# Two heads' attention scores side by side in 64-row halves of TensorE, and softmax sums from a column of ones

## The chip, the cores and the metric

One Trainium2 chip, one of its cores. The metric is the time of one execution on the device in microseconds (us), as the median of several executions. Inside the core five engines run their own instruction lists and wait for each other through semaphores: TensorE (PE in the profile, with its weight loads as PEld), VectorE (DVE), ScalarE (ACT), GpSimd (POOL) and SyncE (SP), from which nearly all DMAs are issued.

## The reference

One encoder block on 1024 tokens of width 1024. A projection gives queries, keys, values and gates for two groups of eight heads of width 64. Group A attends in a 2-D neighbourhood (16 rows by 64 columns of tokens, a window of 8 rows by 16 columns, a learned bias); group B attends in a band of 128 tokens to either side, with rotary positions, two heads of keys and values for eight of queries, and a learned sink logit per head. Both are gated, projected back, added to the input and normalised.

```python
# group A: neighbourhood
s = jnp.einsum('bqhd,biqjhd->bhqij', q_r, k_win).astype(jnp.float32) * scale
s = s + bias.astype(jnp.float32)[None]
p = jax.nn.softmax(s.reshape(B, H, GRID_W, kh * kw), axis=-1).reshape(B, H, GRID_W, kh, kw)
return jnp.einsum('bhqij,biqjhd->bqhd', p.astype(v.dtype), v_win)
...
# group B: band with a sink
s = jnp.einsum('bnqkgd,bnjkd->bnkgqj', qb, k_band).astype(jnp.float32) * (D ** -0.5)
s = jnp.where(valid[None, :, None, None], s, MASK_VALUE)
p = jax.nn.softmax(jnp.concatenate([s, sink_col], axis=-1), axis=-1)[..., :-1]
out = jnp.einsum('bnkgqj,bnjkd->bnqkgd', p.astype(v.dtype), v_band)
...
mixed = jnp.concatenate([y_a * jax.nn.silu(z_a), y_b * jax.nn.silu(z_b)], axis=-1)
y = jnp.einsum('bse,ed->bsd', mixed, w_out[layer])
x = layer_norm(DEEPNORM_ALPHA * x + y, ln_gain[layer], ln_bias[layer])
```

## The kernel before

Everything is float32 outside. For TensorE each operand is split into two float16 parts, a high one and a low one (h and l in the names), and a product of two matrices is made as the sum of high times high, high times low and low times high.

The kernel has three stages. The first (to about 121 us) makes the values `v` and the first six of 21 projections. The second is the attention, 128 units long, and the third, from about 372 us, is the output projection with the normalisation. The change lies in the second stage and in what prepares it.

A unit (`unit_list`) is 128 queries of one head: group B first, then group A; four pairs `p` of heads in each; within a pair the two heads `j`, and for each the eight blocks `t` of 128 queries. Group A's tokens are sorted by column, so that one block is eight columns of 16 rows. A block's keys lie in the two or three blocks around it, so a unit's scores are 128 by 384, or 128 by 256 for the first and the last block (`geom`).

The loop at the end of `hybrid_block` goes over the units; its counter is called a step. In step `i`:

- `stage_qk` (L777) makes the scores of unit `i` in a PSUM bank of four (tag `s`). Of each head there is a `qs` tile whose 128 rows are 64 rows of q's high part and 64 of its low part, and two `ks` tiles: k's high part twice, one over the other, and its low part twice. So two matmuls with all 128 rows contracted give all four products (L797, L798). Then DVE adds bias or mask and takes the row's extreme in one instruction (L805), out of PSUM into one of two `sn` tiles. For group B a DVE copy puts the sink in column 384 of `sn` (L802).
- `stage_exp` (L811) is ACT's exponential, back into the same PSUM bank, with the row sum as a second result (`accum_out`, read by an instruction of its own).
- `stage_tr` of unit `i - 1` scales the probabilities and splits them in a high part (ACT, L829) and a low part (DVE, L830), and SP issues a DMA that transposes both (L833).
- Every fourth step `stage_pv` (L840) multiplies the transposed probabilities of four earlier units with `v`: for each block of keys three matmuls of 64 columns (L856). One step later `stage_on` (L858) divides by the row sums, and `stage_ot` (L868) transposes pairs of heads with TensorE (L876) and multiplies them onto the gate (L879 group B, L882 group A).
- Between them `pump_to` issues matmuls of the remaining 15 projections (`project`, L380), 48 each, as many as `FILL_AT` says for the step, and later the first ones of the output projection (L1002). When a projection is done, its result is copied out of PSUM: `split_q` and `split_k` write the `qs` and `ks` tiles. For each head and half of the tokens that is an ACT instruction (L250 or L252) and a DVE one (L256; for rotary heads POOL, L258) on 64 partitions, and for keys two POOL copies (L298), which fill the other 64 rows. These instructions stand in queues of work (`enq`, `pop`) and are issued a few per step; `need` issues at once what is still missing when a unit begins.

The first stage's `v_part` (L683) splits `v`; group A's goes to DRAM (`vd`) with 256 numbers for a pair of heads, and `gather_v` (L736) fetches it in the order of columns. Within a step the order of the instructions on each engine is the order of these calls; no scheduler changes it.

Of the kernel before, what the change touches and what calls it, by code (L numbers as in the profile page):

```python
# [27 lines left out]
LTT, LPP, BP, BH, BR, ND, NA, NX, F1 = 1, 6, 2, 9, 5, 1, 1, 6, 0.2  # L28
# [7 lines left out]
FILL_AT = [0, 8, 17, 25, 33, 41, 49, 57, 66, 74, 81, 89, 97, 105, 112, 121, 123.5, 126, 128, 131, 136]  # L36
# [5 lines left out]
VA_STEP = (0, 1, 1)  # L42
# [8 lines left out]
BWIN = (0, 256, 640, 896)  # L51
# [4 lines left out]
def hybrid_block(ctx, tc, xT, x, wt, wv, wo, bias, sink, gain, lbias, cos, sin, bmask, out):  # L56
# [15 lines left out]
    vd = dram.tile([4, GW, ROWS, 256], F16, name="vd")  # L72
# [57 lines left out]
    def stk(kind):  # L130
        if kind == "q":
            return tiles["kq"].tile([128, S], F16, tag="qs", name="qs", bufs=4)
        return tiles["kq"].tile([128, S], F16, tag="ks", name="ks", bufs=8)
# [108 lines left out]
    def own(kind, p, j):  # L242
        if (kind, p, j) not in stks:
            stks[kind, p, j] = stk(kind)
        return stks[kind, p, j]
# [16 lines left out]
    def place(t, a, half, by_col):  # L262
        if not by_col:
            return t[a, 512 * half:512 * half + 512]
        return t[a].rearrange("p (c r) -> p c r", r=ROWS)[:, :, 8 * half:8 * half + 8]

    def taken_from(src, a, by_col):
        return src[a].rearrange("p (r c) -> p c r", c=GW) if by_col else src[a]

    def split_q(p, half, src, dep=None):  # L270
        col = dep is None
        ops = []
        prio = 0 if dep is None else 1
        eng = "pool" if dep and clock["step"] is not None else "dve"
        for j in range(2):
            a, o = slice(64 * j, 64 * j + 64), slice(64 - 64 * j, 128 - 64 * j)
            hi, lo = split_hl(lambda j=j, a=a: place(own("q", p, j), a, half, col),
                              lambda j=j, o=o: place(own("q", p, j), o, half, col),
                              taken_from(src, a, col), dep is None, eng)
            o1 = enq("act", hi, dep, prio=prio, after=28 if dep else 0)  # L280
            ops.append(enq(eng, lo, o1, prio=prio, after=32 if dep else 0))
            stk_ops.setdefault((p, j, half), []).append(ops[-1])
        return ops

    def split_k(p, half, src, dep=None):
        col = dep is None
        ops = []
        prio = 0 if dep is None else 1
        eng = "pool" if dep and clock["step"] is not None else "dve"
        for j in range(2):  # L290
            a, o = slice(64 * j, 64 * j + 64), slice(64 - 64 * j, 128 - 64 * j)
            hi, lo = split_hl(lambda j=j, a=a: place(own("kh", p, j), a, half, col),
                              lambda j=j, a=a: place(own("kl", p, j), a, half, col),
                              taken_from(src, a, col), dep is None, eng)

            def dup_(w, j=j, a=a, o=o):
                t = own(w, p, j)
                nc.gpsimd.tensor_copy(place(t, o, half, col), place(t, a, half, col))  # L298

            o1 = enq("act", hi, dep, prio=prio, after=28 if dep else 0)  # L300
            o2 = enq(eng, lo, o1, prio=prio, after=32 if dep else 0)
            ops.append(o2)
            dup = [enq("pool", lambda d=dup_: d("kh"), o1, after=32 if dep else 0),
                   enq("pool", lambda d=dup_: d("kl"), o2, after=36 if dep else 0)]
            stk_ops.setdefault((p, j, half), []).extend(dup)
        return ops
# [14 lines left out]
    def evac(name, half, ps):  # L321
# [4 lines left out]
        if kind in ("kb", "qb"):  # L326
            raw, o1, o5 = rope(ps, half)
            if kind == "kb":
                split_k("b", half, raw, o5)
            else:  # L330
                split_q(f"b{p}", half, raw, o5)
            return [o1]
        if kind == "k":
            return split_k(p, half, ps)
        if kind == "q":
            return split_q(p, half, ps)
# [69 lines left out]
    with ExitStack() as vctx:  # L406
# [276 lines left out]
        def v_part(t):  # L683
            if t > 0:
                vt, v3 = vts.pop(t - 1)
                nc.vector.scalar_tensor_tensor(vt[:, :, 1, :], v3, vrs, vt[:, :, 0, :], op0=ALU.mult, op1=ALU.subtract)
                nc.vector.tensor_copy(vb[:, t - 1], vt[:, 8:10])
# [4 lines left out]
            if t < 8:  # L692
                vt = vp.tile([128, 10, 2, HD], F16, tag=("vt", "wvr")[t % 2], name=f"vt{t}", bufs=3)
                v3 = v32[t].rearrange("p (h e) -> p h e", e=HD)
                nc.scalar.activation(vt[:, :, 0, :], v3, AF.Copy, scale=vrs)
                vts[t] = vt, v3
# [39 lines left out]
    def gather_v(p):  # L736
        t = va[p] = big_ap([128, 8, 256], F16, f"va{p}")
# [3 lines left out]
    def unit_list():  # L741
        us = []
        for g in "ba":
            for p in range(4):
                for j in range(2):
                    for i in range(8):
                        us.append((g, p, j, i))
# [4 lines left out]
    sns = [ap.tile([128, 388], F32, name=f"sn{i}", bufs=1) for i in range(2)]  # L752
# [7 lines left out]
    def geom(u):  # L760
        g, p, j, t = u
        lo, hi = max(t - 1, 0), min(t + 2, 8)
        return 128 * (hi - lo), hi - lo
# [13 lines left out]
    def stage_qk(u):  # L777
        g, p, j, t = u
        n, _m = geom(u)
        ps = bank("s")  # L780
        lo = max(t - 1, 0) * 128
        if g == "a":
            q = stks["q", p, j][:, 128 * t:128 * t + 128]
            sl = [stks[w, p, j][:, lo:lo + n] for w in ("kh", "kl")]
# [5 lines left out]
        else:  # L790
            q = stks["q", f"b{p}", j][:, 128 * t:128 * t + 128]
            kv = p // 2
            sl = [stks[w, "b", kv][:, lo:lo + n] for w in ("kh", "kl")]
# [3 lines left out]
        nc.tensor.matmul(ps[:, :n], q, sl[0], start=True, stop=False)  # L797
        nc.tensor.matmul(ps[:, :n], q, sl[1], start=False, stop=True)  # L798
        s0 = sns[units.index(u) % 2]
        sn = s0[:, 384 - n:]  # L800
        if g == "b" and t < 2:
            nc.vector.tensor_copy(s0[:, 384:385], nsk[:, h:h + 1])  # L802
# [8 lines left out]
    def stage_exp(u):  # L811
        n, _c = geom(u)
        m = n + 1 if u[0] == "b" else n
# [3 lines left out]
        if k == 0:  # L817
            st["sm"] = ap.tile([128, 4], F32, tag="sm", name="sm", bufs=4)
        sm = st["sm"]
        st[units.index(u) // 4, "sm"] = sm  # L820
        nc.scalar.activation(pt[:, :m], sn[:, :m], AF.Exp, bias=nm, scale=-1.0, accum_out=sm[:, k:k + 1])  # L821
        st[u, "p"] = pt

    def stage_tr(u):
# [3 lines left out]
        src = pt[:, :n].rearrange("p (k c) -> p k c", c=128)  # L828
# [11 lines left out]
    def stage_pv(q):  # L840
        ps = st[q, "o"] = bank("t")
        for m in range(4):
# [4 lines left out]
            for i in range(geom(u)[1]):  # L847
                k = max(t - 1, 0) + i
                if g == "a":
                    v = [va[p][:, k, 128 * j + 64 * e:128 * j + 64 * e + 64] for e in range(2)]  # L850
                else:
                    v = [vb[:, k, p // 2, e, :] for e in range(2)]
                ph, pl = tr[:, 2 * i, :], tr[:, 2 * i + 1, :]
                mms += [(ph, v[0]), (ph, v[1]), (pl, v[0])]
            for i, (a, b_) in enumerate(mms):
# [439 lines left out]
```

## Time and profile before

| | |
|---|---|
| time, median of 3 | 450.94 us (450.64 to 451.16) |
| the profiled execution's own time | 448.97 us |
| its span in the profile, first to last instruction | 447.2 us |
| mean granted TensorE clock | 0.997 |
| HBM traffic | 41.23 MB read, 6.29 MB written |
| DMA, mean | 159 GB/s |

How to read the views: a page gives busy times of the engines, and the same in 40 equal slices of the span, in tenths. A row that groups instructions has line, engine, operation, output and inputs, rows x elements and type, how many (x), then the busy time in us and the mean duration of one in ns, then the engine's idle time ahead of them and what ended it. A row of the timeline has start and duration in us, and in brackets the idle time ahead of it. A matmul's duration holds its way through the array and into PSUM, in which the next one already runs: what a matmul costs TensorE is the distance from its start to the next one's start. A group row's busy time of PE therefore counts more than the matmuls cost.

### The profile page before, as it was taken

The numbers are of one execution on the slowest core, as the hardware profiler recorded it, in microseconds if no ns is written. First come the engines' busy times: TensorE is split into PE (matmuls) and PEld (weight loads), VectorE is DVE, ScalarE is ACT, GpSimd is POOL, SyncE is SP. The second block draws the span as 40 slices with busy tenths as digits, with TensorE's granted clock in tenths as the row PEclk, the third lists the DMA queues.
The fourth block names the chain that finished last, engine by engine and source line by source line (L and its number), as shares of the span: only waits on it lengthen the run. The fifth ranks groups of instructions, "written<-read, shape, count | busy, mean of one in ns | idle before, by whom it ended". The sixth has DMA issues, their size and how long they took to land.

```text
span 447.2 us, 9320 instructions
## 1 busy us (share of the span) xinstructions
PE 437.1 (98%) x3241; PEld 252.9 (57%) x3241; DVE 349.0 (78%) x840; ACT 309.9 (69%) x700; POOL 212.0 (47%) x219
## 2 busy tenths in 40 slices
PE   9999999999999999999999999999979999999995
PEld 8997754444445565555555655555536654444454
DVE  5978867438977898887898888888778847679944
ACT  5759789766599987877867887788777957012401
POOL 0110064637749559766424757565462404304740
PEclk9999999999999999999999999999999999999998
DMA  8921569980169999596986669569669598102711
GB/s 269 391 89 59 170 233 327 319 269 25 53 141 197 212 197 175 105 159 123 166 120 116 130 143 172 93 135 200 131 131 188 102 188 320 47 1 83 247 72 71
DMA packets 123984, 71.21 MB, mean 159 GB/s; under 512 B 96800, under 2 KB 105888, under 8 KB 123936
## 3 DMA queue, kind: packets, MB, share of 16 engines
q1 hardware_dynamic: 123792, 70.48, 65.8%
q8 instruction: 25, 0.41, 0.4%
q14 instruction: 23, 0.19, 0.2%
q10 hardware_dynamic: 144, 0.13, 0.1%
HBM read 41.23 MB, written 6.29 MB: 106 GB/s over the span
## 4 chain that ended last, share of the span: by engine, by line
PE 77%; DVE 10%; ACT 7%; issue 5%; DVEq 0%; ACTq 0%
PE ps_pj L380 36%; PE ps_s L1002 8%; PE ps_s L487 6%; PE ps_pj L1002 5%; PE ps_t L856 5%; PE ps_pj L487 3%; PE ps_t L487 3%; PE ps_t L1002 3%; PE ps_s L797 3%; PE ps_s L798 3%; ACT split L829 3%; ACT ps_s L821 2%; DVE split L830 2%; DVE qs L256 2%; DVE ks L256 1%
## 5 line engine op out<-in xcount | busy, mean ns | idle before, releaser
L380 PE MATMUL ps_pj<-xf,wh 128*128 128x512 f16 x672 | 202.1, 379 | 0.4 <-DVE ks L256 0.4
L380 PE MATMUL ps_pj<-xf,wl 128*128 128x512 f16 x336 | 127.3, 379 | 0.0
L380 PEld LDWEIGHTS <-wh 128*128 128x128 f16 x672 | 63.6, 98 | 61.6 <-DVE ks L256 1.2
L830 DVE SCALAR_TENSOR_TENSOR split<-ps_s,split 128x384 f16<-128x384 f32 (+1 forms) x128 | 66.9, 522 | 28.9 <-ACT split L829 27.5
L821 ACT ACTIVATE ps_s<-sn,nm 128x385 f32<-128x385 f32 (+3 forms) x128 | 71.0, 554 | 26.3 <-DVE nm L805 25.6
L1002 PEld LDWEIGHTS <-m 128*128 128x128 f16 x432 | 40.0, 98 | 41.6 <-DVE m L910 0.7
L829 ACT ACTIVATE split<-ps_s 128x384 f16<-128x384 f32 (+1 forms) x128 | 58.6, 458 | 2.4
L380 PEld LDWEIGHTS <-wl 128*128 128x128 f16 x336 | 32.8, 98 | 37.5
L197 POOL TENSOR_SCALAR wr<-wr,wsc 128x512 f32<-128x512 f32 x26 | 20.5, 789 | 67.7 <-ACT wh L192 61.2
L797 PE MATMUL ps_s<-ks,qs 128*128 128x384 f16 (+1 forms) x128 | 40.0, 313 | 2.9 <-DVE qs L256 2.9
L805 DVE CUSTOM_DVE_ANT_0 sn<-ps_s,bm,nsk 128x384 f32<-128x384 f32 (+1 forms) x64 | 40.7, 636 | 1.4 <-PE ps_s L798 1.2
L1002 PE MATMUL ps_s<-wo,m 128*128 128x512 f16 (+1 forms) x192 | 40.7, 366 | 0.2 <-DVE m L910 0.2
L798 PE MATMUL ps_s<-ks,qs 128*128 128x384 f16 (+1 forms) x128 | 40.0, 313 | 0.0
L805 DVE CUSTOM_DVE_ANT_0 sn<-ps_s,bias,sg 128x384 f32<-128x384 f32 (+1 forms) x64 | 37.0, 578 | 2.6 <-PE ps_s L798 2.0
L856 PEld LDWEIGHTS <-tr 128*128 128x128 f16 x1056 | 35.2, 98 | 2.5
L198 POOL TENSOR_TENSOR wl<-wr,wh 128x512 f16<-128x512 f32 x26 | 32.7, 1256 | 2.2
L298 POOL COPY ks<-ks 64x512 f16<-64x512 f16 x40 | 26.1, 661 | 10.3 <-DVE ks L256 3.4
L197 POOL TENSOR_SCALAR ws<-ws,wsc 128x512 f32<-128x512 f32 x16 | 11.1, 691 | 33.9 <-ACT wh L192 30.1
L1002 PE MATMUL ps_pj<-wo,m 128*128 128x512 f16 (+1 forms) x144 | 26.5, 326 | 0.0
L1101 POOL TENSOR_TENSOR xr<-xr,gb 128x512 f32<-128x512 f32 x7 | 9.8, 1396 | 32.5 <-ACT xr L1098 32.5
L821 ACT ACTIVATION_READ_ACCUMULATOR ps_s<-sn,nm 128x1 f32 x128 | 24.4, 191 | 0.0
L797 PEld LDWEIGHTS <-qs 128*128 128x128 f16 x128 | 12.5, 98 | 18.4 <-DVE qs L256 3.4
(187 smaller groups left out, 800.2 us busy)
## 6 DMA issues: line engine op xcount, KB each, us to landing
ws<-in_wt SPq DMA_DIRECT2D x15, 512.0 KB, 5.8
wr<-in_wt SPq DMA_DIRECT2D x26, 256.0 KB, 3.8
wor<-in_wo SPq DMA_DIRECT2D x22, 256.0 KB, 3.5
xr<-in_x SPq DMA_DIRECT2D x8, 512.0 KB, 9.0
out<-xr SPq DMA_DIRECT2D x15, 256.0 KB, 2.1
bias<-in_bias SPq DMA_DIRECT2D x8, 448.0 KB, 3.9
wvraw<-in_wv SPq DMA_DIRECT2D x9, 320.0 KB, 5.9
xraw<-in_xT SPq DMA_DIRECT2D x11, 256.0 KB, 4.5
```

The costliest lines, as they stand in the source:

```text
L197: nc.gpsimd.tensor_scalar(raw, raw, scale, 1.0, op0=ALU.mult, op1=ALU.mult)
L198: nc.gpsimd.tensor_sub(l, raw, h)
L380: nc.tensor.matmul(ps, a[:, k % 4, :], mv, start=(k == 0 and i == 0), stop=(k == KT - 1 and i == 2))
L487: nc.tensor.matmul(ps[:, :320], lh[:, ts], rh[:, cs], start=(k == ko[0] and i == 0), stop=(k == ko[-1] and i == 2))
L797: nc.tensor.matmul(ps[:, :n], q, sl[0], start=True, stop=False)
L798: nc.tensor.matmul(ps[:, :n], q, sl[1], start=False, stop=True)
L805: nc.vector.tensor_tensor_reduce(sn[:, :n], ps[:, :n], bias_t, sg[:, c:c + 1], init, op0=ALU.add, op1=ALU.min, accum_out=nm)
L821: nc.scalar.activation(pt[:, :m], sn[:, :m], AF.Exp, bias=nm, scale=-1.0, accum_out=sm[:, k:k + 1])
L829: nc.scalar.activation(hl[:, :m, 0, :], src, AF.Copy, scale=PSCALE)
L830: nc.vector.scalar_tensor_tensor(hl[:, :m, 1, :], src, PSCALE, hl[:, :m, 0, :], op0=ALU.mult, op1=ALU.subtract)
L856: nc.tensor.matmul(ps[:, HD * m:HD * m + HD], a, b_, start=(i == 0), stop=(i == len(mms) - 1))
L1002: nc.tensor.matmul(ps, lh[:, ts], rh[:, cs], start=(e == EO[0] and i == 0), stop=(e == EO[-1] and i == 2))
```

## The change

The scores. The `qs` tiles now hold q's high part for both heads of a pair (64 rows each), and its low part, and the `ks` tiles likewise; `split_qk` takes the place of `split_q` and `split_k` and works on all 128 partitions at once. The copies into the other 64 rows are gone, except for group B's keys (`split_kb`), which four heads share. The units of a pair alternate between the heads, and at the even one `stage_qk` makes the scores of both: three products for each head, each contracting 64 rows, the two heads in turn in the upper and the lower half of the array, into two PSUM banks. The product of the low parts is left out.

```diff
+HALVES = (slice(0, 64), slice(64, 128))
...
-                for j in range(2):
-                    for i in range(8):
-                        us.append((g, p, j, i))
+                for t in range(8):
+                    us.extend((g, p, j, t) for j in range(2))
...
-        ps = bank("s")
-        lo = max(t - 1, 0) * 128
+        if j == 0:
+            banks = [bank("s") for _ in range(2)]
+            lo = max(t - 1, 0) * 128
+            kp = p if g == "a" else f"b{p // 2}"
+            qp = p if g == "a" else f"b{p}"
+            for i, (a, b) in enumerate((("qh", "kh"), ("qh", "kl"), ("ql", "kh"))):
+                for c, ps in zip(HALVES, banks):
+                    nc.tensor.matmul(ps[:, :n], stks[a, qp][c, 128 * t:128 * t + 128], stks[b, kp][c, lo:lo + n],
+                                     start=(i == 0), stop=(i == 2))
+            st["banks"] = banks
+        ps = st["banks"][j]
...
-        nc.tensor.matmul(ps[:, :n], q, sl[0], start=True, stop=False)
-        nc.tensor.matmul(ps[:, :n], q, sl[1], start=False, stop=True)
...
+    def split_qk(kind, p, half, src, dep=None):
+        col = dep is None
+        prio = 0 if dep is None else 1
+        eng = "pool" if dep and clock["step"] is not None else "dve"
+        hi, lo = split_hl(lambda: place(own(kind + "h", p), half, col), lambda: place(own(kind + "l", p), half, col),
+                          src.rearrange("p (r c) -> p c r", c=GW) if col else src, col, eng)
+        o1 = enq("act", hi, dep, prio=prio, after=28 if dep else 0)
+        o2 = enq(eng, lo, o1, prio=prio, after=32 if dep else 0)
+        stk_ops.setdefault((p, half), []).append(o2)
+        return [o2]
...
-            if u[0] == "a" and u[3] == 0:
-                need(*stk_ops[u[1], u[2], 0], *stk_ops[u[1], u[2], 1])
+            if u[0] == "a" and u[3] == 0:
+                need(*stk_ops[u[1], 0], *stk_ops[u[1], 1])
```

The sums. For group A, `v`'s high part gets a 65th column of ones, and the two products with it become 65 columns wide, so that the row sum comes out of `stage_pv`; the exponential there has no second result. Group B keeps it.

```diff
-    vd = dram.tile([4, GW, ROWS, 256], F16, name="vd")
+    vd = dram.tile([4, GW, ROWS, 4 * VE], F16, name="vd")
...
+                nc.gpsimd.memset(vt[:, 0:8, :, HD:VE], 1.0 / PSCALE)
...
-        nc.scalar.activation(pt[:, :m], sn[:, :m], AF.Exp, bias=nm, scale=-1.0, accum_out=sm[:, k:k + 1])
+        acc = st[units.index(u) // 4, "sm"][:, k:k + 1] if u[0] == "b" else None
+        nc.scalar.activation(pt[:, :m], sn[:, :m], AF.Exp, bias=nm, scale=-1.0, accum_out=acc)
...
-                    v = [va[p][:, k, 128 * j + 64 * e:128 * j + 64 * e + 64] for e in range(2)]
+                    v = [va[p][d, k, VE * (2 * j + e):VE * (2 * j + e) + (VE, HD)[e]] for e in range(2)]
...
-                mms += [(ph, v[0]), (ph, v[1]), (pl, v[0])]
+                mms += [(ph, v[0], w), (ph, v[1], HD), (pl, v[0], w)]
...
-        nc.vector.reciprocal(ri, st.pop((q, "sm")))
+        nc.vector.reciprocal(ri, o[:, :, HD] if g == "a" else st.pop((q, "sm")))
```

Smaller edits. A group A unit with three blocks of keys has 368 score columns instead of 384 (a window of 16 columns cannot reach the last one), and its third block in `stage_pv` contracts 112 rows. There are four `sn` tiles instead of two, and the sink is put there by POOL some steps ahead. The gate product of group A runs over rows outside and columns inside. Eight `ks` buffers become six. `FILL_AT`, by which the projections are spread over the steps, and the step of `gather_v` are set anew.

```diff
-FILL_AT = [0, 8, 17, 25, 33, 41, 49, 57, 66, 74, 81, 89, 97, 105, 112, 121, 123.5, 126, 128, 131, 136]
+FILL_AT = [0, 8, 16, 24, 32, 40, 48, 55.5, 63, 70.5, 78, 85.5, 93, 101, 109, 121, 123.5, 126, 128, 131, 136]
...
-VA_STEP = (0, 1, 1)
+VA_STEP = (1, 2)
...
-    sns = [ap.tile([128, 388], F32, name=f"sn{i}", bufs=1) for i in range(2)]
+    sns = [ap.tile([128, 388], F32, name=f"sn{i}", bufs=1) for i in range(4)]
...
+    def sink_load(i):
+        if i < NU and units[i][0] == "b" and units[i][3] < 2:
+            h = 2 * units[i][1] + units[i][2]
+            nc.gpsimd.tensor_copy(sns[i % 4][:, 384:385], nsk[:, h:h + 1])
...
-        return 128 * (hi - lo), hi - lo
+        m = min(t + 2, 8) - max(t - 1, 0)
+        return 368 if g == "a" and m == 3 else 128 * m, m
...
-            z = zt[p].rearrange("p (r c) -> p c r", c=GW)[:, 32 * h:32 * h + 32, :]
-            nc.vector.scalar_tensor_tensor(z, ps.rearrange("p (c r) -> p c r", r=ROWS), z_col(p), z,
+            z = zt[p].rearrange("p (r c) -> p r c", c=GW)[:, :, 32 * h:32 * h + 32]
+            nc.vector.scalar_tensor_tensor(z, ps.rearrange("p (c r) -> p r c", r=ROWS), z_col(p), z,
                                            op0=ALU.mult, op1=ALU.mult)
...
-            if g == "a" and p < 3 and (j, h, m) == VA_STEP:
+            if g == "a" and p < 3 and (q % 4, m) == VA_STEP:
```

More of the change, by code (lines that the diff above doesn't have):

```diff
@@ L240, in hybrid_block, with own, place @@
     stks = {}
[L242 to L245, printed above, removed]
+    def own(kind, p):
+        if (kind, p) not in stks:
+            stks[kind, p] = stk(kind[0])
+        return stks[kind, p]
+    def place(t, half, by_col):
+        if not by_col:
+            return t[:, 512 * half:512 * half + 512]
+        return t.rearrange("p (c r) -> p c r", r=ROWS)[:, :, 8 * half:8 * half + 8]
     def split_hl(h, l, src, scaled, eng):
@@ L275, in split_q @@
         for j in range(2):
             a, o = slice(64 * j, 64 * j + 64), slice(64 - 64 * j, 128 - 64 * j)
[L277 to L289, printed above, removed]
-        for j in range(2):
[L291 to L294, printed above, removed]
-            def dup_(w, j=j, a=a, o=o):
[L297 to L306, printed above, removed]
@@ L796, in stage_qk @@
             init = nsk[:, h:h + 1]
[L797 to L802, printed above, removed]
+        s0 = sns[units.index(u) % 4]
+        if g == "a" and p == 0 and t < 2:
+            nc.vector.memset(s0[:, 368:384], -NEG)
+        sn = s0 if g == "a" else s0[:, 384 - n:]
         nm = ap.tile([128, 1], F32, tag="nm", name="nm", bufs=6)
@@ L1149, in gain_load @@
         nc.sync.dma_start(gain_tile[0], gain.partition_broadcast(128))
+    for i in range(4):
+        sink_load(i)
     clock["step"] = 0
```

97 lines of the change are left out of this document (47 added, 50 removed).

## The prediction

> **What bounds the kernel now.** I read the page's busy times first, then TensorE's waits in the attention stage, then its timeline.
>
> ```profile
> PE 437.1 (98%) x3241; PEld 252.9 (57%) x3241; DVE 349.0 (78%) x840; ACT 309.9 (69%) x700; POOL 212.0 (47%) x219
> ...
> PE   9999999999999999999999999999979999999995
> ```
>
> PE is at nine tenths or more in 38 of 40 slices. A busy PE may still be a waiting one, so the waits of PE between 121 and 370 us come next; there are two rows:
>
> ```profile
> PE ps_s L797 <- DVE qs L256: 2.9, 1, 2.9
> PE ps_pj L380 <- DVE ks L256: 0.4, 1, 0.4
> ```
>
> That is 3.3 us of idle time in 249. The timeline of PE around a score pair shows that nothing lies between its instructions:
>
> ```profile
> 156.12 0.38 PE L380 MATMUL ps_pj<-xf,wl 128*128 128x512 f16 x1
> 156.34 0.33 PE L797 MATMUL ps_s<-ks,qs 128*128 128x384 f16 x1
> 156.50 0.33 PE L798 MATMUL ps_s<-ks,qs 128*128 128x384 f16 x1
> 156.66 0.60 PE L876 MATMUL ps_t<-identf,on 128*128 128x128 f32 x4
> 157.10 1.12 PE L856 MATMUL ps_t<-vb,tr 128*128 128x64 f16 x33
> 158.06 0.38 PE L380 MATMUL ps_pj<-xf,wh 128*128 128x512 f16 x1
> ```
>
> From start to start a 512-column product costs 0.22 us, a 384-column score product 0.16, one of the 33 products with v 0.029 ((158.06 - 157.10) / 33). The duration of the score product is 0.33, so its tail of 0.17 runs under the next. PE's issue sets the time, and a slot saved on PE is time saved, as long as the other engines keep up. How near they are shows in a stretch of group A:
>
> ```profile
> 293.52 0.33 PE L797 MATMUL ps_s<-ks,qs 128*128 128x384 f16 x1
> 299.24 0.27 PE L797 MATMUL ps_s<-ks,qs 128*128 128x256 f16 x1
> 300.12 0.56 DVE L830 SCALAR_TENSOR_TENSOR split<-ps_s,split 128x384 f16<-128x384 f32 x1 [0.36 <-ACT split L829]
> 300.75 0.33 PE L797 MATMUL ps_s<-ks,qs 128*128 128x384 f16 x1
> ```
>
> Counted from the first of their line these are unit 93's scores, unit 96's, the end of unit 93's work (L830 frees its PSUM bank at 300.68) and unit 97's scores, which need that bank: 0.07 us to spare. The chain DVE, ACT, ACT, DVE runs 7 us behind PE there, just not late.
>
> **Score products, the main term.**
>
> ```profile
> L797 PE MATMUL ps_s<-ks,qs 128*128 128x384 f16 x96 | 31.3, 326 | 0.0
> L798 PE MATMUL ps_s<-ks,qs 128*128 128x384 f16 x96 | 31.3, 326 | 0.0
> L797 PE MATMUL ps_s<-ks,qs 128*128 128x256 f16 x32 | 8.7, 273 | 2.9 <-DVE qs L256 2.9
> ...
> 329.02 0.27 PE L797 MATMUL ps_s<-ks,qs 128*128 128x256 f16 x1
> 329.13 0.27 PE L798 MATMUL ps_s<-ks,qs 128*128 128x256 f16 x1
> ```
>
> Now 192 products at 0.16 and 64 (L798's 32 with L797's) at 0.11 cost 30.7 + 7.0 = 37.8 us. After, two units need three slots in place of four if the halves run at the same time: a quarter less, 9.4 us. In group A 24 pairs have 368 columns: 24 x 3 x 0.16 x 16/384 = 0.5. Together **-9.9**.
>
> No row shows products in halves, nor a change between whole and halved array, of which there are 128 (in and out, 64 times). Bounds for one change: nothing, since a change of another kind costs nothing (f16 scores, f32 transposes, f16 products follow at 156.50, 156.66 and 157.10 without a gap); and the whole tail of the product before, 0.17, if the array must run empty, plus a weight load that can't run ahead:
>
> ```profile
> L797 PEld LDWEIGHTS <-qs 128*128 128x128 f16 x128 | 12.5, 98 | 18.4 <-DVE qs L256 3.4
> ```
>
> another 0.10. The nearest row is the change without a gap. Still, the second half starts after the first and ends after it, so I take one bare issue slot, 0.029, for each: 128 x 0.029 = **+3.7** (ends 0 and 34.6). The Trainium skill, "TensorE: Matmul & The Clock Gate", "Part 3: Packing small matmuls", gives about 4 ns between starts of products in different row groups; with it for the 0.029, the sum would be 3.2 us lower. No run here shows it.
>
> **Products with v.** Of group A's 528, 352 become 65 columns wide: 352 x 0.029/64 = **+0.2**. In 144 the contraction has 112 rows; a shorter one is not in the trace: nothing to 144 x 0.029 = 4.2; I take 0, as each product has its own weight load now too.
>
> **The late split.** The 2.9 us wait:
>
> ```profile
> 330.53 0.38 PE L380 MATMUL ps_pj<-xf,wl 128*128 128x512 f16 x1
> 333.11 0.68 DVE L256 SCALAR_TENSOR_TENSOR qs<-ps_pj,qs 64x512 f16<-64x512 f32 x1 [0.68 <-ACT qs L250]
> 333.85 0.28 PE L797 MATMUL ps_s<-ks,qs 128*128 128x256 f16 x1 [2.94 <-DVE qs L256]
> ```
>
> The last projection of q ends with step 112, at which its pair begins, and four splits on two engines come behind it. After, it ends at step 109, three steps (over 5 us) ahead, with one split in place of two for each half. The wait goes, and the 0.4 with it: **-3.3**. What is late next is the bank, below.
>
> **ACT, DVE and POOL.** These give the chain room, no time by themselves, as PE is what issues late.
>
> ```profile
> L256 DVE SCALAR_TENSOR_TENSOR qs<-ps_pj,qs 64x512 f16<-64x512 f32 x16 | 11.0, 688 | 1.1 <-ACT qs L250 0.7
> L256 DVE SCALAR_TENSOR_TENSOR ks<-ps_pj,ks 64x512 f16<-64x512 f32 x16 | 11.0, 686 | 0.3
> L250 ACT ACTIVATE qs<-ps_pj 64x512 f16<-64x512 f32 x16 | 9.4, 585 | 5.5 <-DVE qs L256 5.5
> L821 ACT ACTIVATION_READ_ACCUMULATOR ps_s<-sn,nm 128x1 f32 x128 | 24.4, 191 | 0.0
> L802 DVE COPY sn<-nsk 128x1 f32<-128x1 f32 x16 | 2.3, 145 | 0.0
> L298 POOL COPY ks<-ks 64x512 f16<-64x512 f16 x40 | 26.1, 661 | 10.3 <-DVE ks L256 3.4 <-ACT ks L250 3.0 <-PE ps_s L798 1.3
> L882 DVE SCALAR_TENSOR_TENSOR z<-ps_t,zc,z 128x512 f32<-128x512 f32 x8 | 9.3, 1168 | 7.4 <-PE ps_t L876 7.4
> L879 DVE SCALAR_TENSOR_TENSOR z<-ps_t,zc,z 128x512 f32<-128x512 f32 x8 | 6.0, 747 | 0.0
> ```
>
> DVE loses half of L256 (11.0) and L802 (2.3), between 0 and 3.4 in L882 (its row against L879's); ACT loses as much as half of L250 (9.4 with the keys' row) and 64 of 128 reads (12.2); POOL loses 32 of 40 copies (21) and gains 16 of one column. POOL's new copies wait for ACT's exponential of the unit before; behind them stand the weight splits, and POOL is 47% busy. If that cover fails, a projection starts late by one lag of the chain, some 4 us at most.
>
> **The bank, a new wait.** Scores of two units go out at the even step, so unit 97's would go out with unit 96's, at 299.24, and its bank comes free at 300.68: 1.4 us late in this trace. PE would stand, and behind it the projections of that step. Ends: 0, if the chain's relief shortens its lag, and once in each of eight pairs, 11. The relief is the nearer row (11.0 of DVE): I take a little under one such wait for each group, **+2.0**.
>
> **The thin stretch.** Steps 109 to 121 now carry one projection, 48 products in 12 steps. PE's step: 4 x 0.216 (the first row below, of the chain of waits, has 16 in 3.45 us) + 0.26 of scores ((3 x 0.156 + 2 x 0.029) / 2) + 33 x 0.029/4 + 0.06 of transposes (0.44 at 156.66, every eighth step) = 1.42 us. DVE's are the other rows:
>
> ```profile
> 117.97 3.45 PE ps_pj L380 x16
> ...
> L805 DVE CUSTOM_DVE_ANT_0 sn<-ps_s,bias,sg 128x384 f32<-128x384 f32 x48 | 29.3, 611 | 1.8 <-PE ps_s L798 1.4
> L830 DVE SCALAR_TENSOR_TENSOR split<-ps_s,split 128x384 f16<-128x384 f32 x96 | 53.4, 556 | 24.3 <-ACT split L829 23.2 <-POOL wl L198 0.4
> L805 DVE DVE_READ_ACCUMULATOR2_ANT nm<- 128x1 f32 x128 | 10.6, 83 | 0.0
> L865 DVE TENSOR_TENSOR on<-ps_t,ri 128x256 f32<-128x256 f32 x32 | 13.6, 424 | 2.4 <-PE ps_t L856 1.3
> L862 DVE RECIPROCAL ri<-sm 128x4 f32<-128x4 f32 x32 | 5.4, 168 | 0.0
> ```
>
> 0.61 + 0.56 + 0.08, a quarter of 0.42 and of 0.17, and an eighth of L882's 1.17 make 1.54. DVE is the slower one: 12 x 0.12 = **+1.5** (ends 0 and, if the wait comes in bursts, twice that).
>
> **The sum.** -9.9 + 3.7 + 0.2 - 3.3 + 2.0 + 1.5 = -5.8. The profiled execution took 448.97, so 443.2; the median of the runs is 1.97 above that execution, which I add: **445.1 us**.
>
> **The rivals.**
>
> *The array runs empty at every change of its division* (slower). Place: first score product of a pair, and first whole product behind it. For it speaks the tail of 0.17 in each product; against it the f32 change without a gap. Without any price for changes the kernel would take 441.4, so it decides from (450.94 - 441.4) / 128 = 0.075 us a change. At 0.17 a change costs 21.8 in place of 3.7; with a slower PE the chain no longer blocks, -3.5: 445.1 + 18.1 - 3.5 = 459.7, and up to 472 with the weight load. The Trainium skill, "TensorEngine Tiling (Array Packing)", "Key Properties", states it as a rule: changing the tiling mode, not only the tile, drains TensorE. It gives no price, and no trace here has such a change.
>
> *The halves don't run at the same time*, so the change doesn't do what it says: six slots for two units, 37.8 x 1.5 - 1.0 = 55.7, +17.9 in place of -9.9: 445.1 + 27.8 - 3.5 = 469. The two write different banks and have weights of their own, which speaks against it; no row shows either.
>
> *The chain takes the place of PE.* Units 57 to 110 have 0.07 to 2 us to spare now; if the chain gets no faster there, PE's gain stays in the 44 steps ahead and in the late split: -3.3 - 44 x 0.077 + 3.7 = -3.0, 448. For it speaks the 0.07; against it DVE's 11 us less, over some 90 steps 0.12 a step, more than PE's 0.08.
>
> *Everything hidden*: changes free, no bank wait, no thin stretch: -9.9 - 3.3 + 0.2, 437.9.
>
> **How the numbers follow.** Forecast 0.46 (own range 441 to 450), running empty 0.24, chain 0.12, halves in turn 0.09, everything hidden 0.09. The range holds the first, the chain, half of the cheapest and most of running empty: 439.5 to 463. This measurement tells 0.2%, 0.9 us, from no change. Faster: 0.43 + 0.11 + 0.09 = 0.63; slower: 0.23 + 0.09 = 0.32; the same: 0.05, what is left of the three.
>
> **What would show it.** Between the six score products of a pair, starts that come in twos, the twos 0.16 apart, and 0.5 us from the first to the next whole product; the step fails with six starts 0.16 apart, or with gaps of over 0.075 ahead of the first and behind the last. L256 with 128 rows, x16. No wait of PE at unit 112. Waits of the score products for L830, 2 us in all, and from step 109 to 121. I am wrong if PE's idle time, or the distance at the changes, is more than the quarter saved.

## The result, and the profile after

The changed kernel takes 452.18 us (median of 20 runs, 450.79 to 453.42), the kernel before 451.17 on the same chips (20 runs, 448.84 to 452.91): a ratio of 1.0027, 95% interval 1.0015 to 1.0039. It is slower by about a quarter of a per cent, where 445.1 was forecast. The time lies in the range given only because that was drawn wide enough to take in the slower rivals; the forecast's own range ended at 450. The profiled execution of after took 453.12 us with a span of 451.1. That of before (448.97) lay 2.2 under its median, so the two traces are 4.15 apart where the medians differ by 1.0.

From the page of after, the busy engines and PE in 40 slices:

```profile
PE 442.6 (98%) x3369; PEld 238.6 (53%) x3369; DVE 330.9 (73%) x810; ACT 290.3 (64%) x612; POOL 187.1 (41%) x205
...
PE   9999999989999999999999999999999999999995
```

PE is as full as before, with 128 products more. The waits of PE in after (engine, tile and line, what ended the wait, us in total, times, longest):

```profile
PE ps_t L220 <- ACT junk L214: 2.0, 1, 2.0
PE ps_t L1078 <- ACT dr L1076: 1.8, 1, 1.8
PE ps_t L399 <- DVE warm L122: 1.0, 1, 1.0
PE ps_s L778 <- DVE split L821: 0.4, 1, 0.4
```

The 2.9 us at unit 112 is gone and the bank costs 0.4 in all, but a wait of 2.0 stands in the first stage that before didn't have. At the score products themselves only the 0.4 is waited. What they cost shows in the timeline around a pair (start, duration):

```profile
202.29 0.38 PE L366 MATMUL ps_pj<-xf,wl 128*128 128x512 f16 x1
202.61 0.34 PE L778 MATMUL ps_s<-ks,qs 64*128 64x384 f16 x2
...
202.94 0.33 PE L778 MATMUL ps_s<-ks,qs 64*128 64x384 f16 x2
203.20 0.39 PE L366 MATMUL ps_pj<-xf,wh 128*128 128x512 f16 x1
```

Two things are to be seen. The two halves do run together: by the starts in the trace the second follows the first after 2 to 5 ns, and the six products take 0.59 us from the first start to the next whole product, where six slots in turn would take 6 x 0.16 = 0.97. And each end of the group has a gap. A 512-column product is followed by the next one's start after 0.22; here the first half product comes 0.32 behind it. The last round of halves (202.94) is followed by a whole product after 0.26, where a 384-column product takes 0.16. Over all 64 groups the starts give 96 ns (median; 93 to 97) too much going in and 92 (90 to 94) coming out, with 256, 368 and 384 columns alike: 6.1 + 5.9 = **12.0 us for 128 changes, 0.094 each**. This is what the prediction named as its step's failure: gaps over 0.075 ahead of the first and behind the last. PE is called busy in them; no list of its waits shows them.

The groups of after that answer to the rows of before:

```profile
L798 DVE CUSTOM_DVE_ANT_0 sn<-ps_s,bias,sg 128x368 f32<-128x368 f32 x48 | 28.5, 595 | 18.9 <-PE ps_s L778 18.9
...
L778 PE MATMUL ps_s<-ks,qs 64*128 64x384 f16 x144 | 15.9, 326 | 0.0
...
L812 ACT ACTIVATION_READ_ACCUMULATOR ps_s<-sn,nm 128x1 f32 x64 | 12.1, 190 | 0.0
...
L878 DVE SCALAR_TENSOR_TENSOR z<-ps_t,zc,z 128x512 f32<-128x512 f32 x8 | 6.0, 750 | 6.6 <-PE ps_t L872 6.6
...
L263 DVE SCALAR_TENSOR_TENSOR qs<-ps_pj,qs 128x512 f16<-128x512 f32 x8 | 5.5, 682 | 0.0
```

L256's splits of 688 ns on 64 rows became L263's of 682 on 128, half as many. The gate product went from 1168 to 750 ns, half of the reads of row sums are gone. DVE's score instruction of group A's longer units now waits 18.9 us for PE, where it waited 1.8. Over the attention stage, 121 to 370 us, the windows of before and of after (length; busy time and count of PE, PEld, DVE, ACT, POOL; granted clock, DMA share, GB/s):

```profile
121.00:370.00 249.00, 245.67 (x2160) 139.54 (x2159) 203.78 (x552) 200.40 (x506) 136.69 (x147) 1.00 0.80 151
```

```profile
121.00:370.00 249.00, 248.65 (x2256) 122.90 (x2254) 187.83 (x522) 181.73 (x420) 114.79 (x127) 1.00 0.81 146
```

DVE, ACT and POOL lost 16, 19 and 22 us of work, and none of it shows as time, because PE sets the pace: it waits 0.4 us in that stretch.

### The profile page after: what moved, and what is told of

It reads as the page before. It is cut to its first block, busy times and chain, and to the rows that moved or that the text cites. A ratio compares the mean times of both kernels' runs of the same rounds, so it can differ in the third digit from the quotient of the medians.

```text
span 451.1 us, 9373 instructions
## 1 busy us (share of the span) xinstructions
PE 442.6 (98%) x3369; PEld 238.6 (53%) x3369; DVE 330.9 (73%) x810; ACT 290.3 (64%) x612; POOL 187.1 (41%) x205
## 4 chain that ended last, share of the span: by engine, by line
PE 89%; DMA 4%; ACT 2%; issue 2%; POOL 1%; DVE 1%; SPq 1%; POOLq 0%; ACTq 0%
PE ps_pj L366 41%; PE ps_s L998 9%; PE ps_s L778 8%; PE ps_t L850 7%; PE ps_s L473 6%; PE ps_pj L998 5%; PE ps_t L998 5%; PE ps_pj L473 3%; PE ps_t L473 3%; DMA vd<-vt 2%; DMA ws<-in_wt 2%; PE ps_t L872 1%; POOL split L740 1%; PE ps_t L399 1%; SPq L675 0%
## 5 line engine op out<-in xcount | busy, mean ns | idle before, releaser
L366 PEld LDWEIGHTS <-wh 128*128 128x128 f16 x672 | 60.6, 98 | 77.9 <-issue 17.1
L798 DVE CUSTOM_DVE_ANT_0 sn<-ps_s,bias,sg 128x368 f32<-128x368 f32 (+1 forms) x64 | 36.2, 565 | 23.9 <-PE ps_s L778 23.8
L798 DVE CUSTOM_DVE_ANT_0 sn<-ps_s,bm,nsk 128x384 f32<-128x384 f32 (+1 forms) x64 | 40.7, 637 | 13.1 <-PE ps_s L778 12.9
L778 PE MATMUL ps_s<-ks,qs 64*128 64x368 f16 (+2 forms) x384 | 39.6, 310 | 0.4 <-DVE split L821 0.4
L850 PEld LDWEIGHTS <-tr 128*128 128x128 f16 (+1 forms) x1056 | 36.2, 98 | 4.2
L778 PEld LDWEIGHTS <-qs 64*128 64x128 f16 x384 | 13.7, 94 | 30.8 <-issue 27.3
L1053 ACT ACTIVATE sd<-mv,eps 128x1 f32<-128x1 f32 x8 | 2.4, 294 | 37.8 <-DVE mv L1051 36.5
L965 POOL TENSOR_SCALAR wor<-wor,wos 128x512 f32<-128x512 f32 x9 | 8.9, 994 | 36.0 <-DVE wo L957 21.7
L998 PE MATMUL ps_t<-wo,m 128*128 128x512 f16 x96 | 22.8, 379 | 0.0
```

What stands on the lines that cost most here:

```text
L366: nc.tensor.matmul(ps, a[:, k % 4, :], mv, start=(k == 0 and i == 0), stop=(k == KT - 1 and i == 2))
L778: nc.tensor.matmul(ps[:, :n], stks[a, qp][c, 128 * t:128 * t + 128], stks[b, kp][c, lo:lo + n], start=(i == 0), stop=(i == 2))
L798: nc.vector.tensor_tensor_reduce(sn[:, :n], ps[:, :n], bias_t, sg[:, c:c + 1], init, op0=ALU.add, op1=ALU.min, accum_out=nm)
L850: nc.tensor.matmul(ps[:, w * m:w * m + e], a, b_, start=(i == 0), stop=(i == len(mms) - 1))
L998: nc.tensor.matmul(ps, lh[:, ts], rh[:, cs], start=(e == EO[0] and i == 0), stop=(e == EO[-1] and i == 2))
```

## The experiments

Two theories stood after the result (A and B of e1 and e2). *Changes:* the 0.094 us at each change of the array's division is the whole loss, the rest of the forecast sum is about right. *Other costs:* the gaps only show where another cost lands (the chain behind PE, the ones' column, the moved projections), and taking the changes away gains little.

**e1, twice as many changes.** One projection product is issued in the middle of the six, so that the array changes four times for a pair. The amount of work is the same.

```diff
                                      start=(i == 0), stop=(i == 2))
+                if i == 0:
+                    pump(1)
+                    pumped[0] += 1
```

> In every pair one projection product is moved from behind the six half-array score products into their middle, after the first two: the work is the same, but the array's division changes 256 times instead of 128. Theory A (each change costs PE about 0.094 us wherever it stands, the distance that the changed kernel's trace shows ahead of the first and behind the last score product): 128 x 0.094 = 12.0 us more than the changed kernel, about 464 us. Rival B (the distances at the changes are not a price of the change, but a wait for the other engines that shows there, because the score products are the ones with waits): no or hardly any more time, 452 to 453 us.

464.06 us (463.45 to 464.69), ratio 1.0295 (1.026 to 1.033). Its timeline around a pair:

```profile
199.64 0.38 PE L366 MATMUL ps_pj<-xf,wl 128*128 128x512 f16 x1
199.95 0.34 PE L778 MATMUL ps_s<-ks,qs 64*128 64x384 f16 x2
200.22 0.39 PE L366 MATMUL ps_pj<-xf,wh 128*128 128x512 f16 x1
200.54 0.50 PE L778 MATMUL ps_s<-ks,qs 64*128 64x384 f16 x4
200.98 0.39 PE L366 MATMUL ps_pj<-xf,wh 128*128 128x512 f16 x1
```

Each distance across a change has its gap again: 0.31 and 0.32 going in (0.22 without), 0.27 coming out after one round (0.16 without). The 256 changes cost 12.9 + 12.5 = 25.4 us by the starts, 13.4 more than in after, and the median rose by 11.9. From the first to the last score product the trace of e1 takes 251.0 us, that of after 237.4, which is 13.6 more; ahead of them some of it comes back, as the attention starts at 121.7 us in e1 and at 124.0 in after. The price goes with the number of changes.

**e2, whole products.** The six half products become three of the whole array, of the same columns, into the same two banks. Two banks then hold sums over both heads, so the scores are not the reference's; the number of columns streamed, the splits, the chain and the moved projections are those of after.

```diff
-                for c, ps in zip(HALVES, banks):
-                    nc.tensor.matmul(ps[:, :n], stks[a, qp][c, ...], stks[b, kp][c, lo:lo + n], start=(i == 0), stop=(i == 2))
+                nc.tensor.matmul(banks[i % 2][:, :n], stks[a, qp][:, ...], stks[b, kp][:, lo:lo + n], start=(i < 2), stop=(i > 0))
```

> The six half-array score products of a pair become three of the whole array with the same columns, into the same two banks; the scores are then not those of the reference. Slots of PE as after the change, but no change of the array's division. Theory A: the 12.0 us at the changes go, 440 us (and if the first stage's 2.7 us stay, the rest of the kernel runs as fast as PE can issue). Rival B (the other engines can't keep up with a faster PE: banks, the thin stretch from step 109): PE waits appear in place of the changes, 446 us or more.

441.38 us (440.56 to 442.03), ratio 0.9791 (0.9761 to 0.982): 10.8 under after's median. The timeline and the waits of PE:

```profile
197.17 0.38 PE L366 MATMUL ps_pj<-xf,wl 128*128 128x512 f16 x1
197.38 0.65 PE L777 MATMUL ps_s<-ks,qs 128*128 128x384 f16 x3
197.87 0.59 PE L366 MATMUL ps_pj<-xf,wh 128*128 128x512 f16 x2
```

```profile
PE ps_t L849 <- DMA tr<-split: 1.7, 1, 1.7
PE ps_s L777 <- DVE split L820: 1.6, 3, 0.8
```

From the projection's start to the next one behind the pair it is 0.70 us here and 0.91 in after (202.29 to 203.20); before, the four score products with the projection ahead of them took 0.22 + 4 x 0.16 = 0.86. So three slots do beat four, and two changes cost more than the slot they save. The waits that the forecast feared, for the bank and for the chain, appear here, 1.6 and 1.7 us: they come when PE is faster than in after. With them the changes account for 12.0 + 0.4 - 3.3 = 9.1 of the difference, and from the first to the last score product e2 takes 228.1 us against 237.4, 9.3 less. The two traces differ by another 2.5 us ahead of the attention, which starts at 121.5 us in e2.

**e3, no ones' column.** The first stage's new wait (L220) made me look at the transfers ahead of it. The chain of waits of after, some of its pieces from the first stage (start, duration, what):

```profile
71.22 8.64 DMA vd<-vt
...
88.47 8.45 DMA ws<-in_wt
...
97.01 1.16 ACT junk L691 x2
```

The transfers of `v` to DRAM (L675) and the weights behind them on SP's queue stand on the chain that sets the end; in before PE alone is on it there. The row of DMA issues (count, KB each, median us from issue to landing), after:

```profile
vd<-vt SPq DMA_DIRECT2D x16, 130.0 KB, 7.3
```

Before it reads 128.0 KB and 4.9. With the column, a row of `vd` is 520 bytes; its packets took 35.1 ns on average, those of 512 bytes 28.2. In e3 `v` has no column, ACT makes group A's row sums as in before, and all else is as in after:

```diff
-    vd = dram.tile([4, GW, ROWS, 4 * VE], F16, name="vd")
+    vd = dram.tile([4, GW, ROWS, 256], F16, name="vd")
...
-        acc = st[units.index(u) // 4, "sm"][:, k:k + 1] if u[0] == "b" else None
+        acc = st[units.index(u) // 4, "sm"][:, k:k + 1]
...
-            w = VE if g == "a" else HD
+            w = HD
```

> The changed kernel without the column of ones: v's rows in DRAM are 512 bytes again instead of 520, products with v 64 columns wide, group A's exponential gives the row sums again. Theory A (rows of 520 bytes are slower to write, the loads behind them land later, and TensorE waits 2.2 us for the weights' scale near 102 us): that wait goes, attention starts near 121.3 us instead of 124.0, 449.5 us. Rival B (that wait is chance of one execution or comes from something else): attention starts near 124 again, time within 0.5 us of the changed kernel's, or 1 to 2 us more, if ACT's 64 extra reads make the chain late.

449.7 us (12 runs), ratio 0.9981 (0.9964 to 0.9997). No wait at L220, and the row is before's again:

```profile
vd<-vt SPq DMA_DIRECT2D x16, 128.0 KB, 4.8
```

The attention's first score product starts at 121.9 us, in after at 124.0. ACT does 64 more reads of 190 ns, and the time shows nothing of them.

**e7, rows of 576 bytes.** If the length of the rows alone decides, a still longer row is worse; if 520 is an awkward length, 576 may be better. The column stays; each row is filled up with more ones.

```diff
+VS = 72
...
-    vd = dram.tile([4, GW, ROWS, 4 * VE], F16, name="vd")
+    vd = dram.tile([4, GW, ROWS, 4 * VS], F16, name="vd")
...
-                nc.gpsimd.memset(vt[:, 0:8, :, HD:VE], 1.0 / PSCALE)
+                nc.gpsimd.memset(vt[:, 0:8, :, HD:VS], 1.0 / PSCALE)
```

> The changed kernel with the rows of v in DRAM made 576 bytes long (a multiple of 64) instead of 520, the rest of the row filled with the same constant. [...] Rival B (any longer row is slower, or it is the order of the loads): 576-byte packets take 37 ns or more and the last row lands at 93 us or later, 452 us or more.

450.33 us (12 runs), ratio 1.0001 (0.9981 to 1.002), no wait at L220, and with 11% more bytes the transfers land earlier:

```profile
vd<-vt SPq DMA_DIRECT2D x16, 144.0 KB, 4.7
```

Its packets took 31.6 ns, in proportion to 512 bytes at 28. The column by itself makes no wait; the row of 520 bytes is what the traces with a long wait have and this one hasn't. The longer mean comes from a few slow packets: of 4096, 232 took over 60 ns with 520 bytes, 40 with 576 and 18 with 512, while the median packet took 28, 29 and 27. Why that length is slow no run shows.

**f1, f2, f3: after, e7 and e3 again, together.** So far the three had been measured on different chips beside different runs of before, and the differences were near their spread.

> The changed kernel once more, on one chip with the next two, since the first profile of it has a wait of 2.2 us in the first stage that the traces of e1_more_changes and e2_whole_products show with 0.3 to 0.4 us only. Theory A (520-byte rows leave the weights' scale late, by an amount that varies from execution to execution): PE waits for the scale again, 0.3 to 2.5 us, and the last row of v lands at 92 us or later. Rival B (that wait was chance, the rows do nothing): no such wait, the last row lands near 89 us.

> e7_rows_576 once more beside f1_after_again. Theory A: 1.0 to 2.0 us less than f1_after_again. Rival B (the rows cost nothing in time): within 0.5 us of it.

> e3_no_ones once more beside both. Theory A (0.5 us for the 65 columns and the 112 rows on top of the rows): 0.3 to 0.8 us less than f2_rows_576_again. Rival B (the wider products cost nothing): the same as f2_rows_576_again within 0.2 us.

On one chip, 12 runs each beside before's 450.98: after 452.5, ratio 1.0041 (1.0019 to 1.0063); 576-byte rows 450.5, ratio 1.0002 (0.9981 to 1.0024); no column 449.76, ratio 0.9989 (0.9972 to 1.0006). By these medians the row's length costs 2.0 us (1.2 by the ratios of the first runs of after and of e7), and the column itself, with its 352 products of 65 columns, 0.7 more. In f1's execution of after the wait, of 2.0 in the first one, is

```profile
PE ps_t L220 <- ACT junk L214: 1.5, 1, 1.5
```

and the attention starts at 122.8, in the trace with 576 bytes at 122.2. The wait varies from execution to execution: e1 and e2 have the same 520-byte rows (34.5 and 35.6 ns a packet, the last one at 91.0 and 90.7 us, against 92.8 and 92.2 in the two traces of after and 88.3 and 90.0 with 576 bytes), but e2 waits 0.1 us at L220, and e1 this long:

```profile
PE ps_t L220 <- ACT junk L214: 0.3, 1, 0.3
```

So how much of the 2.0 passes through that wait stays open. About 0.4 lies elsewhere: group A's products with `v` are that much shorter with 576-byte rows.

**e4, before with the last projection of q earlier.** Is the late split worth the 2.9 us of its wait? Before's code, with only the due steps of the last projections drawn forward:

```diff
-FILL_AT = [..., 66, 74, 81, 89, 97, 105, 112, 121, ...]
+FILL_AT = [..., 66, 74, 81, 88, 95, 102, 109, 121, ...]
```

> The kernel before, with its last four projections moved ahead so that the last one of q is done at step 109 instead of 112; nothing else. Theory A (the 2.9 us wait at unit 112 is lost time of the kernel before and needs no new scores to go): 447.5 to 448.5 us. Rival B (the chain of the other engines has no room for projections that come closer together, and the wait moves to the score products' banks): 450.5 us or more.

449.26 us (12 runs), ratio 0.9973 (0.9956 to 0.999): 1.5 us under before, between the two expectations. The wait at unit 112 is gone, and others are there:

```profile
PE ps_pj L1002 <- DVE z L345: 1.1, 1, 1.1
...
PE ps_pj L380 <- DVE qs L256: 0.7, 1, 0.7
```

Of the 2.9 us, 1.8 come back in these two. The projections that were brought forward leave less to do for the steps behind them, and the output projection (L1002) then waits for the last gate. That is my reading of the two rows; it wasn't tried by itself.

**e5, four units at once.** If changes cost 0.094, half as many should save 6 us. Four banks then fill together, so the exponential has to leave PSUM: it goes to a tile in SBUF. The ones' column is out, as in e3.

```diff
-        if j == 0:
+        if j == 0 and t % 2 == 0:
...
+            for t2 in (t, t + 1):
...
-        st[u, "ps"] = ps
+        st[u, "ps"] = ap.tile([128, 388], F32, tag="pt", name="pt", bufs=2)
```

> The kernel of e3_no_ones with the scores of four units (two blocks of both heads) made in one go, at every fourth step, so that the array's division changes 64 times instead of 128; the exponential then writes to SBUF, as all four PSUM banks are needed again four steps later. Theory A (0.094 us a change): 64 x 0.094 = 6.0 us less than e3_no_ones, 443.7 us, which is less than both kernels. Rival B (the four banks are needed all at once, and VectorE's read of the last unit comes too late): PE waits for banks of 0.1 us or more at each of the 32 groups, and the time stays at 447 us or above.

452.85 us (10 runs), ratio 1.0057 (1.003 to 1.0084), 3 us slower than e3. The 64 changes cost 3.1 + 2.9 = 6.0, just half; but PE now waits for DVE to have read the banks:

```profile
PE ps_s L780 <- DVE nm L800: 8.0, 7, 1.8
```

and DVE got slower. Its split, which reads the exponential, in e5 and in e3:

```profile
L823 DVE SCALAR_TENSOR_TENSOR split<-pt,split 128x384 f16<-128x384 f32 x96 | 73.5, 766 | 11.3 <-ACT split L822 10.7
```

```profile
L820 DVE SCALAR_TENSOR_TENSOR split<-ps_s,split 128x384 f16<-128x384 f32 x96 | 53.2, 554 | 13.2 <-ACT split L819 12.4 <-POOL wl L200 0.4
```

**e6, the exponential in SBUF alone.** The control for e5: e3 with that one edit.

```diff
-        st[u, "ps"] = ps
+        st[u, "ps"] = ap.tile([128, 388], F32, tag="pt", name="pt", bufs=2)
```

> The control for e5_four_units: e3_no_ones with the exponential written to SBUF and nothing else. Theory A (PE's issue sets the time, the place of the exponential does not): within 0.7 us of e3_no_ones, 449 to 450.4 us. Rival B (writing to SBUF makes ACT or VectorE faster and that is what e5_four_units would gain): 447 us or less.

451.11 us (10 runs), ratio 1.0014 (0.9992 to 1.0035): 1.4 more than e3, over both expectations. Freeing the bank earlier gained nothing; the split takes 719 ns here, and PE waits 1.6 us for DVE ahead of the transposes (L871), which it doesn't in e3. So of e5's loss against e3 the SBUF tile accounts for about 1.4, and the banks, filled four at a time, for more than the 6 us that the fewer changes saved: the wait above is 8.0.

**e8, the old scores with the new sums.** Before with the due steps of e4, the ones' column in 576-byte rows, the new order of the gate product, and one buffer fewer for the splits, which makes room for the longer rows. The scores are made as in before.

```diff
-FILL_AT = [..., 66, 74, 81, 89, 97, 105, 112, 121, ...]
+FILL_AT = [..., 66, 74, 81, 88, 95, 102, 109, 121, ...]
...
-NSPLIT, NP = 6, 2
+NSPLIT, NP = 5, 2
...
-        nc.vector.reciprocal(ri, st.pop((q, "sm")))
+        nc.vector.reciprocal(ri, o[:, :, HD] if g == "a" else st.pop((q, "sm")))
```

> What the runs leave of the change without the halves: the kernel of e4_before_early_q3 (scores of the kernel before, last projection of q three steps earlier) with the column of ones in rows of 576 bytes, the gate product of group A over rows outside, and five split buffers instead of six, for room. Theory A (ACT's 64 reads of sums, 12 us, gave the chain's lag, so the waits of 2.7 us that the earlier projections brought in e4_before_early_q3 go, against 0.2 to 0.5 us for 65 columns): 447 to 448.5 us, less than both kernels. Rival B (those waits come from VectorE, not from ACT, or the longer rows cost as much as they give): 449 us or more.

447.79 us (12 runs, 446.56 to 448.8) beside before's 449.94: ratio 0.9943 (0.9924 to 0.9961), faster than both kernels. The late waits of e4 (1.1 for the last gate, 0.7 for `qs` and 0.4 for `ks`) are smaller, and the one for `qs` is gone:

```profile
PE ps_pj L1007 <- DVE z L347: 0.5, 1, 0.5
...
PE ps_pj L382 <- DVE ks L258: 0.2, 1, 0.2
```

Here the relief of ACT and DVE seems to shorten waits, where in after it bought nothing. Which of the edits does it was not taken apart.

## Why the prediction was wrong

The terms of its sum, with what the trace of after has for each (us):

| term | forecast | measured |
|---|---|---|
| score slots | -9.9 | -9.1 |
| changes of the array's division | +3.7 | +12.0 |
| products with v | +0.2 | +0.9 |
| late split | -3.3 | -3.3 |
| bank wait | +2.0 | +0.4 |
| thin stretch | +1.5 | 0 |
| wait in the first stage, 520-byte rows | not in the sum | +1.5 to +2.0 |
| sum | -5.8 | +2.4 to +2.9 |

The medians moved by +1.0 (by +1.5 in the later runs), the profiled executions by +4.15 and their spans by +3.9, because before's profiled execution lies 2.2 under its median and that of after 0.9 above. The sum is made from the traces, so about a microsecond of the 3.9 stays unassigned.

**The step that failed is the price of a change, "128 x 0.029".** I had bounds, nothing and 0.27, and took one bare issue slot, because the nearest row was a change from f16 to f32 without a gap. That row is of another kind: the whole array stays in use. The measured 0.094 lies beyond the 0.075 from which, by the prediction's own reckoning, the change loses. The rival "the array runs empty at every change" named the place and the sign. Its price, the tail of 0.17, was too high by almost half, 0.096 and 0.092 were measured, and the weight load of 0.10 on top of it is not part of the price. The weight load and the product, on 128 rows without a change, at the wait of unit 112 in before, and going in in after:

```profile
201.89 0.10 PEld L797 LDWEIGHTS <-qs 128*128 128x128 f16 x1
202.10 0.33 PE L797 MATMUL ps_s<-ks,qs 128*128 128x384 f16 x1
...
333.84 0.10 PEld L797 LDWEIGHTS <-qs 128*128 128x128 f16 x1 [3.43 <-DVE qs L256]
333.97 0.27 PE L798 MATMUL ps_s<-ks,qs 128*128 128x256 f16 x1
...
202.60 0.28 PEld L778 LDWEIGHTS <-qs 64*128 64x128 f16 x6 [0.42 <-issue]
```

Usually the load starts 0.21 us ahead of its product. At unit 112, where it waited for its data, and at every change its product starts some 4 ns behind it, and the next one only some 10 ns later than usual (120 ns against 109 at unit 112, 173 against 163 at a change). So a late load costs about 10 ns, and the gap lies ahead of the load, between it and the product before. That fits an array that must run empty first; but no row shows the tail itself, so this part of the mechanism is argued. The Trainium skill, "TensorEngine Tiling (Array Packing)", "Key Properties", states that a change of the tiling mode drains TensorE; by that rule both ends of a group show a gap, and the trace agrees, with 96 and 92 ns. It gives no price, the trace does. I gave the rule 0.24 on the strength of a row that could not speak to it.

A pair of units now costs 0.69 us at 384 columns against 0.65, and 0.53 against 0.436 at 256: the first from the gap going in (0.096) and the 0.594 from first half product to next whole product, the old one from four starts 0.162 (0.109) apart. The price doesn't depend on the columns and the saved slot does, so the short pairs lose most. With 0.19 for two changes and 0.01 for the late second halves, one slot would have to be about 0.20/0.162 x 384 = 470 columns long to pay for them, an estimate from these starts.

**Score slots.** Right in kind. The starts of all score products sum to 38.4 us before; after, without the changes and the 0.4 us wait, to 29.3. The 0.8 that is missing from 9.9 lies in the rounds: three of 384 columns take 502 ns by the starts, not 3 x 162, with a few ns for each second half and some ten for the first round. The Trainium skill, "TensorE: Matmul & The Clock Gate", "Part 3: Packing small matmuls", has about 4 ns there; the trace agrees with 2 to 5. "The halves in turn" is out by the same starts.

**Without any price for changes: 441.4.** e2 is that case and took 441.38. So the rest of the sum held as a whole, though it needed the bank and the thin stretch to do so: e2 has 3.3 us of such waits, the forecast 3.5. That the two numbers meet to 0.02 us is luck: against before, e2 is 9.4 faster by the medians and 8.0 by the profiled executions, where 9.5 was forecast. In after these waits vanish, since a slower PE is what the chain waits for (18.9 us of DVE's row). The prediction had said this of the rival and subtracted 3.5.

**Products with v.** The distances of all 1056 sum to 31.87 against 31.32, and 0.39 of the latter is the wait for `ks`, which the late split already counts: 0.9 more. In e3, without the column, they sum to 31.00, so the column is nearly all of it. The products next to the wider ones grew too: those of 64 columns in group A took 33 ns on average in after, where I had counted the wider ones alone. With 112 rows contracted a product took 30 ns in e3, where I had taken no difference from 29.

**Late split.** The wait is gone, as forecast, but e4 shows that taking it away by itself is worth 1.5 us, not 2.9, at the pace of before.

**What was not seen.** The prediction costed the ones' column in PE's products and on ACT, and never in the DMA that writes `v` to DRAM, though its row becomes 520 bytes. f1 and f2 show that this is worth 2.0 us, and f1 and f3 that the whole column is worth 2.7 in this kernel: without it, the changed kernel is about equal to before (0.9989).

**DVE, ACT and POOL** were relieved as worked out and the relief bought no time in after. "The chain takes PE's place" is out there; in e5 something like it happened, PE waiting 8.0 us for DVE.

## What to carry to other kernels

Packing two 64-row products side by side saves one product's slot for a pair and pays about 0.19 us for going in and out: count the changes of the array's division first, and put enough packed products in a row (here one slot of 384 columns was too little for two changes). Where a change has no row in the trace, the nearest row is only worth as much as it shares the mechanism; if the break-even price lies inside the bounds, the chance belongs near even. When a tile gets one column more, look at every transfer it goes through, not only at the engines.

## What the runs showed of the hardware that was not expected

- A change between products on 128 rows and on 64 costs 0.094 us (96 ns in, 92 ns out, 90 to 97), whatever the number of columns; with a product of another kind in between (e1) it is 101 and 98 on average. PE counts as busy meanwhile. A weight load that comes late costs about 10 ns.
- Rows of 520 bytes written to DRAM took 34.5 to 36.2 ns a packet on average (after, f1, e1, e2), 28.2 at 512 (before) and 30.8 to 31.6 at 576 (f2, e7); the transfers landed after 6.7 to 7.3, 4.9, and 4.7 to 5.3 us (median).
- DVE's split of 128 x 384 takes 554 ns when it reads the float32 exponential from PSUM (e3) and 719 and 766 when that lies in SBUF (e6, e5).
